# All stores of two input projections move from SyncE's queue to ScalarE's

## The chip, the cores and the metric

The kernel runs on one core of a Trainium2 chip. A core has TensorE (matrix products, into PSUM), VectorE, ScalarE and GpSimd for elementwise work, and SyncE (SP), which here only begins DMAs. ScalarE can begin DMAs too. The metric is the device time of one execution in microseconds (us). Before the change the median of 3 runs is 3293.2 us (3289.35 to 3299.78).

## The reference

A two-layer encoder over two requests of 512 and 2048 tokens, model width 1024, float32. Each layer has one input projection, two mixers, gates, one output projection and a layer norm:

```
even: qa,ka,va,qb,kb,vb,ga,gb = split(x @ w_in)
      a = windowed attention with sinks(qa,ka,va);  b = dilated attention, 3 patterns(qb,kb,vb)
      y = concat(a * silu(ga), b * silu(gb)) @ w_out
odd:  qc,kc,vc,qd,id,zf,zb,gc,gd = split(x @ w_in)
      c = 2-D neighbourhood attention(qc,kc,vc);  d = gated linear recurrence, both directions(qd,id,zf,zb)
      y = concat(c * silu(gc), norm(d) * silu(gd)) @ w_out
x <- LayerNorm(ALPHA * x + y)
```

## The kernel before

**Blocks and passes.** The 2560 tokens of both requests are five blocks of 512 (block 0 is the short request). A layer's projection handles output columns in pairs of 128-column units. `group` makes a list of work: first the pairs for blocks 0 and 1, then again for blocks 2 and 3, then for block 4 alone. Most items of the first two passes work on two blocks at once; some at the ends of a pass, and all of the last pass, on one.

**A pair.** `products` computes a pair for a block by seven products instead of eight (Strassen's scheme with shared sums). Each product takes one weight combination, split into a high part and a rest, so that three float32r matmuls stand for one float32 matmul. `next_w` keeps up to six such weight tiles (`whl`) ready. A product's PSUM accumulator is read by ScalarE (`u`, line 280, the first product) or VectorE (lines 272, 274 and those in `fin`), which frees it. There are four accumulators, two in the last pass of each layer.

**Weights.** `weights` loads a pair's weights (`wraw`, lines 178 to 181). In the first pass it builds all seven combinations: ScalarE makes the high part (line 108), GpSimd subtracts it for the rest (line 109). Four of the seven are stored to DRAM (`wk_f`, `wk_v`, line 217). In later passes these four are loaded back (line 206), and only three are built.

**Results.** `fin` ends a unit. VectorE, for gates also ScalarE's sigmoid, writes an `evo` tile; queries and keys of layer 0 are split into `evh` and the rest. Tiles go to DRAM from lines 376 and 378 (feature-major units), 393 (transposed values), 419 and 425 (values of `pair_v`; line 425 issues four stores of 80 KB for each tile). `evo` and `evh` share four buffers in layer 0, three in layer 1; a buffer is written again only when its store has landed.

**Order.** Two hand-written lists (the work list, and generators that slip loads of activations, bias tables and mixer work between products) give the order of the program. A planner then works through the program with its own estimate of durations: each engine takes the earliest instruction of the program whose inputs are ready, and the order found is fixed for each engine and queue. A DMA started by SP or ScalarE stands in that engine's order: it is issued when its inputs are ready and its completion semaphore is free. There are eight such semaphores, given out in turn over the DMAs of both queues, so that a DMA also waits for the one eight places earlier to land. The two mixers of a layer begin before the projection has ended: mixer A of layer 0 and mixer D of layer 1 run beside the last pass.

ScalarE begins only two kinds of DMA, both in the output of layer 0: the new `x` (line 998) and its transpose (line 952). All others, 2,159 of 2,199, are SP's.

Of the kernel before, what the change touches and what calls it, by code (L numbers as in the profile page):

```python
# [9 lines left out]
F32 = mybir.dt.float32  # L10
# [7 lines left out]
P = 128  # L18
# [54 lines left out]
class Trunk:  # L73
# [88 lines left out]
    def weights(self, L, pairs):  # L162


        nc = self.nc

        def load(p, first=False, kept=False):
            src = self.A[f"wv{L}"][p[1]] if p[0] == "v" else self.A[f"w{L}"][2 * p[1]:2 * p[1] + 2].unsqueeze(0)
            raws = []
            for i in range(src.shape[0]):  # L170
                raws.append(self.rp.tile([P, 2, 2, 512], F32, tag="raw", name="wraw"))
                if first:

                    part = lambda m, f, r=raws[i], i=i: nc.sync.dma_start(r[:, m, f], src[i, m, :, f * 512:f * 512 + 512])
                    part(0, 0)
                    rest.extend(lambda m=m, f=f: part(m, f) for m, f in ((0, 1), (1, 0), (1, 1)))
                elif kept:
                    nc.sync.dma_start(raws[i][:, 0].rearrange("p f c -> p (f c)"), src[i, 0])
                    nc.sync.dma_start(raws[i][:, 1, 1], src[i, 1, :, 512:])
                else:  # L180
                    nc.sync.dma_start(raws[i].rearrange("p m f c -> p m (f c)"), src[i].rearrange("m p c -> p m c"))
            return raws

        rest, kept = [], self.kept[L]
        ahead = load(pairs[0], L == 0)
        yield
        for r in rest:
            r()
        for i, p in enumerate(pairs):
            raws, ahead = ahead, None  # L190
            again = p in kept
            if not again:
                kept[p] = [[self.dram.tile([P, 2, 512], F32, name=f"wk{L}_{p[0]}{p[1]}_{j}_{n}") for n in range(4)]
                           for j in range(len(raws))]
            sums = []
            for r in raws if not again else ():
                s = self.rp.tile([P, 2, 512], F32, tag="sum", name="wsum")
                nc.vector.tensor_add(s[:, 0], r[:, 1, 0], r[:, 1, 1])
                nc.vector.tensor_sub(s[:, 1], s[:, 0], r[:, 0, 0])
                nc.vector.tensor_sub(r[:, 1, 0], r[:, 0, 0], r[:, 1, 0])  # L200
                sums.append(s)
            for n in range(7):
                for j, r in enumerate(raws):
                    w = self.wp.tile([P, 2, 512], F32R, tag="w", name="whl")
                    if again and 2 <= n < 6:
                        nc.sync.dma_start(w.bitcast(F32), kept[p][j][n - 2])
                        yield w
                        continue
                    if n == 3:
                        nc.vector.tensor_sub(r[:, 0, 1], r[:, 0, 1], sums[j][:, 1])  # L210
                    if 2 <= n < 6:
                        src = (sums[j][:, 1], r[:, 1, 0], sums[j][:, 0], r[:, 0, 1])[n - 2]
                    else:
                        src = {0: r[:, 0, 0], 1: r[:, 0, 1], 6: r[:, 1, 1]}[n]
                    self.split(w[:, 0], w[:, 1], src, nc.gpsimd)
                    if 2 <= n < 6:
                        nc.sync.dma_start(kept[p][j][n - 2], w.bitcast(F32))
                    yield w
                if n == 1 and i + 1 < len(pairs) and len(raws) == 1 and pairs[i + 1][0] == "f":
                    ahead = load(pairs[i + 1], kept=pairs[i + 1] in kept)  # L220
            if ahead is None and i + 1 < len(pairs):
                ahead = load(pairs[i + 1], kept=pairs[i + 1] in kept)
# [72 lines left out]
    def pair_fm(self, L, p, blocks, xs):  # L295
        nc, ev, nb = self.nc, self.ev, len(blocks)
# [13 lines left out]
        def fin(m, hf, accs, us):  # L310
            n, j = units[m]
# [3 lines left out]
            o = outs[m][:, :, hf]  # L315
            a = accs[0].rearrange("p (b t) -> p b t", t=256)
            u = us[0].rearrange("p (b t) -> p b t", t=256)
            if n[0] in "gz":
                c = ev.tile([P, nb, 256], F32, tag="ev", name="evc", padded_shape=[P, 2, 256])
# [40 lines left out]
            if n in ("va", "v2"):  # L360
                self.late.append(lambda o=outs[m], n=n, j=j: self.transposed(o, n, j, blocks))
            else:
                o, fm = outs[m], self.fm[L][n]
                split = n in SPLIT and not (n in ("qb", "kb") and j > 3)
                if split:
                    h = ev.tile([P, nb, 2, 256], F32, tag="eo", name="evh", bufs=4 - L, padded_shape=[P, 2, 2, 256])
                    self.split(h.bitcast(F32R), o.bitcast(F32R), o, nc.gpsimd if nb > 1 else nc.vector)
                for i, v in ((0, h), (1, o)) if split else ((0, o),):
                    dst = fm[i, j] if n in SPLIT else fm[j]
                    if n in ("qb", "kb") and j // 2 == 1:  # L370

                        for k, b in enumerate(blocks):
                            off, size = REQ[b > 0]
                            rd = dst[:, off:off + size].rearrange("p (r t) -> p r t", r=4)
                            t0 = (b * 512 - off) // 4
                            nc.sync.dma_start(rd[:, :, t0:t0 + 128], v[:, k].rearrange("p f (r t) -> p (f r) t", r=2))
                    else:
                        nc.sync.dma_start(dst[:, blocks[0] * 512:(blocks[-1] + 1) * 512], v.rearrange("p b h t -> p (b h t)"))

        self.products(1, nb * 256, scale, mul, fin)  # L380

    def transposed(self, o, n, j, blocks):

        nc = self.nc
        for i, b in enumerate(blocks):
            pt = self.acc()
            ot = o[:, i].rearrange("p h t -> p (h t)")
            for t in range(4):
                nc.tensor.transpose(pt[:, t * P:(t + 1) * P], ot[:, t * P:(t + 1) * P], self.ident)
            o2 = self.ev.tile([P, 512], F32, tag="ev", name="evt")  # L390
            nc.scalar.activation(o2, pt, AF.Copy)
            dst = self.va if n == "va" else self.vb[:, 512 + 128 * j:640 + 128 * j]
            nc.sync.dma_start(dst[b * 512:b * 512 + 512].rearrange("(j p) c -> p j c", p=P),
                              o2.rearrange("p (j c) -> p j c", c=P))

    def pair_v(self, L, g, blocks, xs):

        nc = self.nc

        def mul(accs, x):  # L400
            w = [self.next_w(), self.next_w()]
            for acc, b in zip(accs, blocks):
                xh, xl = xs[b]
                for t in range(2):
                    for k in range(4):
                        for j, (xv, wi) in enumerate(((xh, 0), (xh, 1), (xl, 0))):
                            nc.tensor.matmul(acc[:, t * 256:(t + 1) * 256], xv[:, k, x, t * P:(t + 1) * P],  # L407
                                             w[k // 2][:, wi, k % 2 * 256:(k % 2 + 1) * 256],
                                             start=(k == 0 and j == 0), stop=(k == 3 and j == 2))

        def fin(m, hf, accs, us):
            for i, b in enumerate(blocks):
                o = self.ev.tile([P, 512], F32, tag="ev", name="evv")
                nc.vector.tensor_add(o, accs[i], us[i])
                o = o.rearrange("p (t c) -> p t c", t=2)
                t0 = b * 512 + hf * 256
                if L == 0 or g:
                    dst = self.vb if L == 0 else self.vd
                    nc.sync.dma_start(dst[t0:t0 + 256, m * 256:(m + 1) * 256].rearrange("(t p) c -> p t c", p=P), o)
                    continue  # L420
                for r in range(2):
                    for h in range(2):
                        p0 = r * 64 + h * 24
                        dst = self.vc[h][t0 // 64 + r:t0 // 64 + r + 3:2, :, m * 256:(m + 1) * 256]
                        nc.sync.dma_start(dst.rearrange("t k c -> k t c"), o[p0:p0 + 40])

        self.products(len(blocks), 512, 1.0, mul, fin)

# [509 lines left out]
    def output(self, L):  # L938
# [16 lines left out]
        for t in range(NT):  # L955
# [41 lines left out]
            if L == 0:  # L997
                nc.scalar.dma_start(self.x1[t0:t0 + P, :], r)
                late.append((t, r))
                if len(late) > 1:  # L1000
                    transposed(*late.pop(0))
# [532 lines left out]
```

## Time and profile before

| | |
|---|---|
| median of 3 runs | 3293.2 us |
| the profiled execution | 3295.48 us |
| its span, first to last instruction | 3293.7 us |
| mean granted TensorE clock (1 is full speed) | 0.963 |
| busy: TensorE, VectorE, ScalarE, GpSimd | 92%, 61%, 41%, 41% |

The projection of layer 0 runs from the start to about 1010 us, beside mixer A from about 760 us. Mixer B and the output of layer 0 follow, then the projection of layer 1 from about 1580 to 2640 us, with mixer D beside it from about 2310 us, then mixers D and C and the output. An engine's idle time is put down to what ended it ("<-"). Idle time of an engine that is not the bottleneck costs nothing. In a row, a name such as `whl<-wk_f` means that `whl` is written from `wk_f`, and SPq and ACTq are the queues of SyncE and ScalarE: their DMA rows last as long as the issue does, not the transfer.

### The profile page before, as it was taken

The page shows a single profiled execution, that of the slowest core. Times are in us where ns is not written, and L with a number is a line of the kernel's source. Part 1 is how long each engine was busy: PE and PEld are TensorE (multiplying, and loading weights), DVE is VectorE, ACT ScalarE, POOL GpSimd, SP SyncE. Part 2 cuts the span into 40 slices and gives each one's busy share as a digit, 9 for nine tenths or more (in the row PEclk, how much of TensorE's full clock was granted, in tenths as well). Part 3 has the DMA queues.
Part 4 walks back from the last instruction along what each step waited for, and adds up shares of the span by engine and source line. Part 5 has one row for each costly group of instructions (what it writes and reads, how often), then busy time and mean ns, then how long its engine had stood idle before and what let it go on. Part 6 is the DMA issues. An engine that isn't in the chain of part 4 may idle for free. (4 is left out here: it accounts for less than half of the span.)

```text
span 3293.7 us, 71171 instructions
## 1 busy us (share of the span) xinstructions
PE 3037.9 (92%) x26922; PEld 2687.0 (82%) x26922; DVE 1999.2 (61%) x4484; ACT 1349.3 (41%) x3179; POOL 1349.4 (41%) x1167
## 2 busy tenths in 40 slices
PE   6999689997998998998899999999899878899998
PEld 5999689986885566677899999999889756667777
DVE  8454543255776665778654564324687988854444
ACT  4333232133555766322433332212343357775551
POOL 6446351332321110375644642113565654543224
PEclk8999899998999999999899999999999989999999
DMA  6857896699998599565855797568979784464443
GB/s 246 292 208 259 284 370 213 225 329 252 305 272 213 131 225 209 141 198 198 321 214 200 263 343 283 197 202 302 321 252 371 233 240 134 141 178 143 150 128 110
DMA packets 518043, 765.31 MB, mean 232 GB/s; under 512 B 72923, under 2 KB 331611, under 8 KB 517447
## 3 DMA queue, kind: packets, MB, share of 16 engines
q1 hardware_dynamic: 494023, 739.79, 70.6%
q10 hardware_dynamic: 23680, 20.97, 2.1%
q8 instruction: 215, 3.52, 0.4%
q14 instruction: 125, 1.02, 0.1%
HBM read 529.09 MB, written 231.54 MB: 231 GB/s over the span
## 5 line engine op out<-in xcount | busy, mean ns | idle before, releaser
L307 PE MATMUL acc<-xh,whl 128*128 128x256 f32 x7560 | 1439.8, 289 | 112.0 <-DMA whl<-wk_f 54.6
L307 PEld LDWEIGHTS acc<-xh,whl 128*128 128x128 f32 x7560 | 1220.5, 196 | 134.8 <-issue 67.6
L307 PE MATMUL acc<-xl,whl 128*128 128x256 f32 x3780 | 1086.4, 287 | 8.0 <-DVE xl L109 8.0
L109 POOL TENSOR_TENSOR whl<-wraw,whl 128x512 fp32r<-128x512 f32 x447 | 613.6, 1383 | 811.9 <-ACT whl L108 773.3
L307 PEld LDWEIGHTS acc<-xl,whl 128*128 128x128 f32 x3780 | 741.8, 196 | 9.5 <-DVE xl L109 9.5
L108 ACT ACTIVATE whl<-wraw 128x512 fp32r<-128x512 f32 x447 | 277.6, 627 | 431.1 <-PE acc L307 167.6
L978 PE MATMUL oacc<-wohl,yh 128*128 128x512 f32 x960 | 321.3, 411 | 1.5 <-ACT yh L108 1.5
L407 PE MATMUL acc<-whl,xh 128*128 128x256 f32 x1680 | 306.7, 285 | 1.4 <-POOL whl L109 1.3
L272 DVE TENSOR_TENSOR u<-acc,u 128x256 f32<-128x256 f32 (+1 forms) x279 | 146.8, 526 | 222.4 <-PE acc L307 138.4
L407 PEld LDWEIGHTS acc<-whl,xh 128*128 128x128 f32 x1680 | 262.9, 192 | 3.7 <-POOL whl L109 1.5
L407 PE MATMUL acc<-whl,xl 128*128 128x256 f32 x840 | 238.4, 284 | 0.0
L978 PEld LDWEIGHTS oacc<-wohl,yh 128*128 128x128 f32 x960 | 181.0, 191 | 46.3 <-issue 2.8
L1249 POOL TENSOR_TENSOR dK<-dK,dT 128x512 f32<-128x512 f32 x120 | 152.2, 1277 | 129.7 <-ACT dKm L1217 78.5
L978 PE MATMUL oacc<-wohl,yl 128*128 128x512 f32 x480 | 195.3, 410 | 0.0
L407 PEld LDWEIGHTS acc<-whl,xl 128*128 128x128 f32 x840 | 161.5, 192 | 0.1
L280 ACT ACTIVATE u<-acc 128x256 f32<-128x256 f32 (+1 forms) x124 | 55.8, 450 | 218.8 <-PE acc L307 189.5
L328 ACT ACTIVATE sg<-evc 128x512 f32<-128x512 f32 (+1 forms) x128 | 70.5, 551 | 181.8 <-DVE evc L320 162.0
L320 DVE TENSOR_TENSOR evc<-acc,u 128x512 f32<-128x512 f32 (+1 forms) x140 | 79.5, 570 | 90.9 <-PE acc L307 83.6
L108 ACT ACTIVATE xh<-xraw 128x768 fp32r<-128x768 f32 (+1 forms) x80 | 73.7, 945 | 143.5 <-DVE xraw L140 87.3
L1094 ACT ACTIVATE css<-css,cm 128x360 f32<-128x360 f32 (+1 forms) x160 | 92.9, 580 | 85.3 <-DVE cm L1092 84.8
L1092 DVE CUSTOM_DVE_ANT_0 css<-cs,ctab 128x360 f32<-128x360 f32 (+1 forms) x160 | 81.2, 509 | 75.0 <-PE cs L1085 72.9
L109 DVE TENSOR_TENSOR xl<-xraw,xh 128x768 fp32r<-128x768 f32 (+1 forms) x80 | 104.0, 1315 | 34.2 <-ACT xh L108 34.1
(1024 smaller groups left out, 5471.4 us busy)
## 6 DMA issues: line engine op xcount, KB each, us to landing
whl<-wk_f SPq DMA_DIRECT2D x328, 512.0 KB
wk_f<-whl SPq DMA_DIRECT2D x108, 512.0 KB
wraw<-w SPq DMA_DIRECT2D x82, 512.0 KB
wraw<-w SPq DMA_DIRECT2D x26, 1024.0 KB
whl<-wk_v SPq DMA_DIRECT2D x48, 512.0 KB
wraw<-w SPq DMA_DIRECT2D x86, 256.0 KB
vtri<-vc_d SPq DMA_DIRECT2D x60, 240.0 KB
bq<-fm_qb SPq DMA_DIRECT2D x50, 256.0 KB
```

Of the source, the lines that this page charges most:

```text
L108: nc.scalar.activation(h, src, AF.Copy)
L109: (eng_l or nc.vector).tensor_sub(l, src, h.bitcast(F32))
L272: nc.vector.tensor_add(d, a, u)
L280: nc.scalar.activation(u[i], a[i], AF.Copy, scale=scale)
L307: nc.tensor.matmul(accs[0][:, i * 256:(i + 1) * 256], w[:, wi, k * P:(k + 1) * P], xv[:, k, x], start=(k == 0 and j == 0), stop=(k == 3 an ...
L320: nc.vector.tensor_add(c, a, u)
L328: nc.scalar.activation(sg, c, AF.Sigmoid)
L407: nc.tensor.matmul(acc[:, t * 256:(t + 1) * 256], xv[:, k, x, t * P:(t + 1) * P], w[k // 2][:, wi, k % 2 * 256:(k % 2 + 1) * 256], start=( ...
L978: nc.tensor.matmul(acc, yv, wo[c][:, wi, cs], start=(c == chunks[0][0] and i == 0), stop=(c == chunks[-1][0] and i == 2))
L1092: nc.vector.tensor_tensor_reduce(ss.rearrange("p (a b) -> p a b", b=40)[:, :nr], sc[:, :nr], tb, 1.0, BIG, ALU.add, ALU.min, m[:, 0:1])
L1094: nc.scalar.activation(ss[:, :nk], ss[:, :nk], AF.Exp, scale=-1.0, bias=m[:, 0:1], accum_out=m[:, 1:2])
L1249: nc.gpsimd.tensor_mul(km, km, of(T_, nb + 1, -(nb + 1), 2, 0))
```

## The change

Six calls that store results or kept weights of the projections are made on `nc.scalar` instead of `nc.sync`. Loads stay on `nc.sync`, and so do all other stores.

```diff
@@ weights
                     if 2 <= n < 6:
-                        nc.sync.dma_start(kept[p][j][n - 2], w.bitcast(F32))
+                        nc.scalar.dma_start(kept[p][j][n - 2], w.bitcast(F32))
@@ pair_fm
-                            nc.sync.dma_start(rd[:, :, t0:t0 + 128], v[:, k].rearrange("p f (r t) -> p (f r) t", r=2))
+                            nc.scalar.dma_start(rd[:, :, t0:t0 + 128], v[:, k].rearrange("p f (r t) -> p (f r) t", r=2))
                     else:
-                        nc.sync.dma_start(dst[:, blocks[0] * 512:(blocks[-1] + 1) * 512], v.rearrange("p b h t -> p (b h t)"))
+                        nc.scalar.dma_start(dst[:, blocks[0] * 512:(blocks[-1] + 1) * 512], v.rearrange("p b h t -> p (b h t)"))
@@ transposed
-            nc.sync.dma_start(dst[b * 512:b * 512 + 512].rearrange("(j p) c -> p j c", p=P),
+            nc.scalar.dma_start(dst[b * 512:b * 512 + 512].rearrange("(j p) c -> p j c", p=P),
@@ pair_v
-                    nc.sync.dma_start(dst[t0:t0 + 256, m * 256:(m + 1) * 256].rearrange("(t p) c -> p t c", p=P), o)
+                    nc.scalar.dma_start(dst[t0:t0 + 256, m * 256:(m + 1) * 256].rearrange("(t p) c -> p t c", p=P), o)
...
-                        nc.sync.dma_start(dst.rearrange("t k c -> k t c"), o[p0:p0 + 40])
+                        nc.scalar.dma_start(dst.rearrange("t k c -> k t c"), o[p0:p0 + 40])
```

## Rows read from the trace of the kernel before

**Rows 1.** The page: busy us, share of the span and instructions of each engine.

```profile
PE 3037.9 (92%) x26922; PEld 2687.0 (82%) x26922; DVE 1999.2 (61%) x4484; ACT 1349.3 (41%) x3179; POOL 1349.4 (41%) x1167
```

**Rows 2.** Windows: stretch, its length, busy us of each engine, granted clock, DMA share, GB/s.

```profile
0.00:100.00 100.00, 66.96 (x417) 61.82 (x418) 79.72 (x93) 39.27 (x61) 60.44 (x46) 0.86 0.73 255
...
300.00:500.00 200.00, 161.03 (x1248) 156.08 (x1247) 105.84 (x170) 62.76 (x105) 93.98 (x71) 0.92 0.95 324
500.00:700.00 200.00, 199.23 (x1658) 198.71 (x1657) 68.97 (x107) 47.02 (x75) 58.68 (x41) 1.00 0.71 242
700.00:1010.00 310.00, 282.28 (x1983) 245.49 (x1982) 207.48 (x579) 148.47 (x381) 82.23 (x146) 0.94 0.96 275
...
2300.00:2640.00 340.00, 305.55 (x4133) 291.42 (x4132) 273.56 (x558) 129.76 (x277) 204.65 (x177) 0.97 0.86 296
```

**Rows 3.** Waits of TensorE, whole span: us in total, times, longest.

```profile
PE acc L307 <- DMA whl<-wk_f: 54.6, 27, 15.8
PE acc L307 <- DVE evo L343: 18.8, 7, 7.1
...
PE acc L307 <- DVE evo L345: 9.3, 5, 6.4
```

**Rows 4.** Timeline of TensorE: start us, duration; [idle before <- what ended it].

```profile
355.56 0.55 PE L307 MATMUL acc<-xh,whl 128*128 128x256 f32 x1 [15.79 <-DMA whl<-wk_f]
...
714.52 0.58 PE L307 MATMUL acc<-xh,whl 128*128 128x256 f32 x1 [6.42 <-DVE evo L345]
...
758.08 0.58 PE L307 MATMUL acc<-xh,whl 128*128 128x256 f32 x1 [7.13 <-DVE evo L343]
```

**Rows 5.** Waits of VectorE, whole span.

```profile
DVE evo L345 <- DMA fm_qb<-evh: 25.5, 7, 7.3
DVE evo L343 <- DMA fm_kb<-evh: 17.1, 3, 10.2
```

**Rows 6.** Issues of four lines: ns min/median/max, first to last start us.

```profile
L217 SPq DMA_DIRECT2D wk_f<-whl x108: 319/320/4970, 23.6 to 1902.3; - x108
...
L378 SPq DMA_DIRECT2D fm_gc<-evo x16: 319/320/2027, 1617.4 to 2639.9; - x16
...
L425 SPq DMA_DIRECT2D vc_d<-evv x80: 273/346/1524, 1796.1 to 2563.6; - x80
...
L998 ACTq DMA_DIRECT2D x_d<-res x20: 326/338/516, 1373.0 to 1577.7; - x20
```

**Rows 7.** Timeline of SP and VectorE, 704 to 758 us.

```profile
704.11 0.84 SPq L378 DMA_DIRECT2D fm_qb<-evh  x2
...
713.88 0.59 DVE L345 SCALAR_TENSOR_TENSOR evo<-acc,u 128x256 f32<-128x256 f32 x1
...
747.98 0.33 SPq L378 DMA_DIRECT2D fm_kb<-evh  x1
...
757.43 0.60 DVE L343 TENSOR_TENSOR evo<-acc,u 128x256 f32<-128x256 f32 x1 [2.93 <-DMA fm_kb<-evh]
```

**Rows 8.** Timeline of SP, 336 to 350 us.

```profile
336.16 4.97 SPq L217 DMA_DIRECT2D wk_f<-whl  x1
341.22 4.95 SPq L178 DMA_DIRECT2D wraw<-w  x1
...
348.26 1.49 SPq L206 DMA_DIRECT2D whl<-wk_f  x2
```

**Rows 9.** Timeline of ScalarE, 1434 us.

```profile
1434.60 0.34 ACTq L998 DMA_DIRECT2D x_d<-res  x1
1434.98 0.59 ACT L799 ACTIVATE cwhl<-cwt 44x512 fp32r<-44x512 f32 x1 [2.35 <-POOL res L993]
```

**Rows 10.** Waits of SP's queue, whole span.

```profile
SPq L217 <- POOL whl L109: 279.2, 102, 21.0
...
SPq L378 <- DMA whl<-wk_f: 7.0, 7, 1.5
```

**Rows 11.** Timeline of SP, 2557 us.

```profile
2557.34 6.53 SPq L425 DMA_DIRECT2D vc_d<-evv  x8
```

## The prediction

> **What bounds the kernel now.** I read the page's busy shares first: TensorE is busy 92% of the span, ScalarE and GpSimd 41% each [rows 1]. ScalarE has room on average; what matters is whether it has room where TensorE waits. The windows say where that is [rows 2]: from 500 to 700 us TensorE misses 0.8 us of 200, so there a store's queue cannot matter to it. It misses 33 us in the first 100, 39 us from 300 to 500, 28 us from 700 to 1010, and 34 us from 2300 to 2640. DMA is near its limit in the second and third of these (0.95 and 0.96).
>
> The waits of TensorE name what ends the idle time [rows 3]: the landing of a kept weight block (54.6 us in 27 waits), and VectorE's `evo` at lines 343 and 345 (18.8 and 9.3 us). Two of the latter are large, 6.42 us at 714.5 and 7.13 us at 758.1; the largest load wait is 15.79 us at 355.6 [rows 4]. Behind `evo` stand the stores: VectorE waited 25.5 and 17.1 us for the landing of `fm_qb<-evh` and `fm_kb<-evh`, whose buffers it wants back [rows 5]. So stores now cost TensorE time in two ways: they land late, and they stand in SP's queue ahead of loads.
>
> **The change part by part.** By the six lines' issue lists 527 stores leave SP (132 of line 217, 40 of 376, 220 of 378, 15 of 393, 40 of 419, 80 of 425), the first at 23.6 us, the last at 2639.9 us [rows 6]. Bytes and shapes stay; only the issuing queue changes, and with it the order that the planner writes down.
>
> *Stores that land late (gain).* The `fm_qb<-evh` pair was issued from 704.11, and `evo` could not start until 713.88; `fm_kb<-evh` was issued at 747.98, and `evo` started at 757.43, a wait that this landing ended [rows 7]. That is over 9 us from issue to reuse, with loads issued ahead of them on the same queue. On a queue that holds stores alone they can pass those loads. Bounds: 13.5 us, if both TensorE waits of rows 4 go; 0, if they land no sooner; and a loss of 5 us, if the loads that are passed land later for it (a tenth of the 54.6 us [rows 3]). Of these I take 7 us, half, because what is late next stands close by: after the wait at 758.1 TensorE needs the next kept block, and DMA is at 0.96 of its time there [rows 2].
>
> The Trainium skill, DMA: Bandwidth & Descriptors, "Issuing engines are not separate DMA queues", speaks against this gain: DMAs begun by several engines end up on the same 16 DMA engines, and beginning them elsewhere saves only the issue time. By it this term would be 0. The same page ("Queues, rings and completion order") says that each DMA engine takes turns between queue rows, which is what would let a store pass; no row of the kernel before shows the two queues side by side under a full load.
>
> *Stores ahead of loads (gain).* At 336.16 SP was held 4.97 us in issuing one `wk_f` store, right behind a store of small pieces at line 493; the weight load behind it then took 4.95 us, and the first kept load came at 348.26, too late for TensorE at 355.6 [rows 8]. With the store gone the load moves up, but it inherits the hold: the weight load that came next was held as long, and line 493 stays on SP. Bounds 0 and 5.0 us; I take 2.5.
>
> *The clock (gain).* The mean granted clock is 0.92 and 0.94 in the two stretches with these waits, 1.00 from 500 to 700 [rows 2]. Where a wait of 6 us goes, the slow restart behind it goes too. Bounds 0 and 6% of 310 us, 19 us; the two gains above are 9.5 of the 67 us idle in these stretches, a seventh, so I take 2 us.
>
> *Issue on ScalarE (loss).* One issue holds the queue 0.32 to 0.35 us at the median, and 0.34 us where ScalarE already issues stores [rows 6]: 527 x 0.34 = 179 us of ScalarE's queue. In the steady stretches TensorE hides it: ScalarE is busy 47 us of 200 from 500 to 700 [rows 2], and its work there (weight splits) is six weight buffers ahead. Cover is thin in the two stretches that work on block 4 alone, where two PSUM accumulators are left and ScalarE's copy `u` frees one of them, while a mixer wants ScalarE too: there it is busy 148 of 310 us and 130 of 340 us [rows 2]. By the code 43 and 48 stores belong to block 4. If all of their issues were on the path it would be 91 x 0.34 = 31 us, if none 0. I take 9 us, three tenths of it, since ScalarE is idle for over half of both stretches.
>
> *Waiting on ScalarE (loss).* ScalarE works in order, so a store that waits for its producer holds what is behind it. The stores at line 998 show it: at 1434.60 one waited for GpSimd, and the activation behind it, which does not need that result, stood 2.35 us [rows 9]. This is 1 of 20 stores there; at the same share 527 / 20 x 2.35 = 62 us of ScalarE, nearly all in its idle time. The stores of line 217 are the most exposed: SP waited 279.2 us for GpSimd at them, in 102 waits [rows 10]. What stands behind them on ScalarE is the split of a later weight block, for which GpSimd and then TensorE wait, five blocks later. Bounds 0 and 62; I take 3 us, most of it in the first 100 us, where TensorE has no blocks in reserve.
>
> Sum: -7 - 2.5 - 2 + 9 + 3 = +0.5 us. The profiled execution took 3295.5 us (its span is 3293.7), 2.3 us above the median of 3293.2. 3295.5 + 0.5 - 2.3 = 3293.7, about 3294: no change that could be told.
>
> **Rivals.**
> *Faster.* Stores pass the loads and SP never stands behind a producer: all `evo` waits go (18.8 + 9.3 = 28.1 us [rows 3]), and the held issue at 336 (5 us), with the clock 5 us, against 9 us of losses: -29 us, 3264. For it: SP's 279 us of waits at line 217 were time in which it could run ahead [rows 10]. Against it: its loads mostly wait for a weight buffer that TensorE still reads, and TensorE loses nothing in the steady stretches.
>
> *Slower, ScalarE held by landings.* The program gives DMAs of both queues eight completion semaphores in turn, and a DMA is issued only when the one eight places earlier has landed: SP's stores at line 378 waited 7.0 us for weight loads that have nothing to do with them [rows 10]. On ScalarE such a wait stops splits and PSUM copies until a load on the other queue has landed, and SP's next loads then wait for that store. Place: the block-4 stretches, above all the `vc_d` stores, eight of which took SP 6.53 us at 2557.34, at a time when mixer D wants ScalarE [rows 11]. Price: 91 stores in eights at 6.5 us are 74 us held; with 40% of it in TensorE's way +30 us, 3323. It decides from about 0.25 us of TensorE time per such store. For it: the last stretch is a chain of short steps over several engines. Against it: the same landings hold TensorE's own loads, so part of the wait is paid now.
>
> *No gain from the second queue.* A store lands no sooner; only the losses stay, +12 us: 3295.5 + 12 - 2.3 = 3305. For it, as a mechanism here: DMA at 0.95 and 0.96, so that what one store gains a load loses [rows 2]. The rule of the Trainium skill that is cited above comes to the same.
>
> *The change does not do what it says.* The eight semaphores tie the two queues together, so that SP runs ahead of the stores by a few DMAs at most and ScalarE's waits fall in its idle time: nothing moves, 3293.
>
> **How the numbers follow.** A measurement of this kernel tells about 0.3% from no change, 10 us, so "same" is 3283 to 3303. Chances: forecast 0.27, change without effect 0.10 (same: 0.37); faster 0.29; ScalarE held 0.24 and no gain 0.10 (slower: 0.34). The range reaches to both outer cases, 3264 and 3323, with 3 us beyond for their own spread: 3261 to 3326. The likeliest case alone spans 3276 to 3305 (its gains doubled and its losses halved, -17 us, or its gains at 0 and its losses at 12).
>
> **What would show it.** In the profile after: the 527 stores stand under ScalarE's queue with medians near 0.34 us. Gain right: VectorE's waits for `fm_qb<-evh` and `fm_kb<-evh` fall well below 42.6 us, and TensorE's for lines 343 and 345 below 28.1 us. Second gain right: the wait at about 355 us shortens by 2 to 3 us. Losses right: new waits of ScalarE behind stores in the block-4 stretches, with TensorE idle there up by some 10 us. The prediction is wrong if ScalarE's waits for unrelated landings reach TensorE, or if TensorE's idle time from 300 to 500 us falls by far more than 3 us.

## The result, and the profile after

The changed kernel takes 3317.3 us (median of 20 runs; 20 runs of the kernel before beside them: 3294.6). The ratio is 1.0064, with a 95% interval of 1.0040 to 1.0087: 21 us slower (13 to 29). That is inside the range, but on the side of the slower cases, not of the case called likeliest. The runs of most kernels here fall into two groups some 30 us apart, the longer ones at a mean granted clock about 0.01 lower (in f1 0.958 to 0.962 against 0.969 to 0.975), and their shares differ from kernel to kernel, so beside the ratio the experiments give the median of the runs within 0.6% of a kernel's fastest, the *lower group*: 3291 before (in every comparison), 3315.5 after.

The profiled execution has a span of 3319.1 us (3293.7 before). The page's busy line, which answers to [rows 1]:

```profile
PE 3043.2 (92%) x26922; PEld 2686.5 (81%) x26922; DVE 1999.1 (60%) x4499; ACT 1337.0 (40%) x3164; POOL 1352.1 (41%) x1167
```

Span less TensorE's busy time is its idle time: 255.8 us before, 275.9 after, 20.1 more. The shares of the other engines hardly move, so the loss cannot be read from them. The windows that answer to [rows 2]:

```profile
0.00:100.00 100.00, 69.30 (x428) 64.49 (x429) 77.77 (x94) 39.75 (x61) 59.68 (x46) 0.95 0.75 264
...
300.00:500.00 200.00, 151.48 (x1122) 146.94 (x1123) 99.75 (x158) 56.36 (x94) 89.05 (x67) 0.88 0.89 296
500.00:700.00 200.00, 199.18 (x1660) 198.89 (x1659) 63.01 (x99) 46.41 (x75) 55.62 (x39) 1.00 0.71 242
700.00:1010.00 310.00, 279.93 (x1956) 240.40 (x1955) 216.22 (x593) 146.13 (x372) 84.92 (x148) 0.96 0.94 276
...
2300.00:2640.00 340.00, 302.20 (x3699) 287.75 (x3699) 254.24 (x520) 123.29 (x255) 191.97 (x164) 0.96 0.87 296
```

Look at 300 to 500 us: TensorE misses 48.5 us instead of 39, and gets through 1122 matrix products instead of 1248. That is the largest single loss, and it lies outside the two block-4 stretches, whose windows lose 2 and 3 us. From 500 to 700 us, as foreseen, nothing moves. (Windows are cut by time, and late work leaves them. By the work itself: three fifths of the first projection's matrix products are done 13 us later than before, at 560.4 us instead of 547.4. The last of them ends 28 us later, at 1041.5, but mixer B, behind it, begins only 14 us later, 13 of which were lost at the three fifths already. The second projection takes 8 us more.) The waits of TensorE, for [rows 3] (total, times, longest):

```profile
PE acc L307 <- ACT u L280: 25.8, 7, 12.1
PE acc L307 <- DMA whl<-wk_f: 22.2, 17, 7.8
PE acc L307 <- DVE evo L345: 15.5, 2, 9.9
...
PE acc L307 <- DVE evo L343: 9.4, 6, 2.7
```

The load wait has fallen from 54.6 to 22.2 us, and a new first line stands above it: ScalarE's PSUM copy `u`, which does not stand among TensorE's waits in the kernel before. VectorE's waits for the two stores of [rows 5] fell from 42.6 to 14.3 us:

```profile
DVE evo L345 <- DMA fm_qb<-evh: 10.3, 3, 4.6
DVE evo L343 <- DMA fm_kb<-evh: 4.0, 1, 4.0
```

What held ScalarE? Two things. The first, in the timeline (start, duration) of SyncE, ScalarE and TensorE of the changed kernel:

```profile
322.01 0.70 SPq L493 DMA_DIRECT2D rz_d<-rp  x1
```

```profile
326.12 4.79 ACTq L376 DMA_DIRECT2D fm_qb<-evh  x1
331.02 0.63 ACT L108 ACTIVATE evh<-evo 128x512 fp32r<-128x512 f32 x1 [4.41 <-issue]
331.32 4.38 ACTq L217 DMA_DIRECT2D wk_f<-whl  x1
335.74 1.35 ACTq L376 DMA_DIRECT2D fm_qb<-evo  x1
...
340.65 0.38 ACT L280 ACTIVATE u<-acc 128x256 f32<-128x256 f32 x1 [9.01 <-issue]
```

```profile
341.09 0.58 PE L307 MATMUL acc<-xh,whl 128*128 128x256 f32 x1 [12.07 <-ACT u L280]
```

SyncE begins the store of line 493 (a bias table, written from 8 partitions). From its semaphore it lands 15.0 us later, at 337.0. Behind it two issues on *ScalarE* take 4.79 and 4.38 us instead of 0.33, and four more 0.8 to 1.4 us each; `u` stands behind all six, and TensorE stands 12.07 us. In the kernel before, the same store slowed the issue of a store and a load on SyncE [rows 8]. The second thing, 35 us later, just behind the second such store (it landed at 363.8):

```profile
374.28 0.33 ACTq L378 DMA_DIRECT2D fm_qb<-evo  x1
375.83 0.33 ACTq L378 DMA_DIRECT2D fm_qb<-evh  x1
376.20 0.84 ACT L108 ACTIVATE xh<-xraw 128x768 fp32r<-128x768 f32 x1 [12.96 <-DMA fm_qb<-evo]
```

```profile
377.08 0.96 DVE L109 TENSOR_TENSOR xl<-xraw,xh 128x768 fp32r<-128x768 f32 x1 [13.03 <-ACT xh L108]
```

```profile
389.27 0.58 PE L307 MATMUL acc<-xh,whl 128*128 128x256 f32 x1 [9.91 <-DVE evo L345]
```

The issues are short here, but each comes 0.08 us after the landing of the DMA eight places earlier, a weight load of SyncE's (by their semaphores these landed at 374.20 and 375.75). ScalarE stands for 12.96 us, VectorE behind it, and TensorE at 389. (The activations that `xh` reads were loaded by SyncE and landed at 368.5, so 7.7 of the 12.96 us at most are the stores' doing.) So a store on ScalarE waits for loads that have nothing to do with it. Going through ScalarE's timeline, I count 35 stores held until the DMA eight places earlier had landed, in three stretches, for 81 us: 25 us from 300 to 500, 35 from 700 to 1010, 22 from 2300 to 2640. All other stretches together have 4 such stores, 6 us. Nearly all of these landings are of SyncE's DMAs; in two of the 39 cases it is an earlier store of ScalarE's own, and the counts below take in both.

### The profile page after: what moved, and what is told of

Same layout as the page of the kernel before. It is cut to its first block, busy times and chain, and to the rows that moved or that the text cites. A ratio compares the mean times of both kernels' runs of the same rounds, so it can differ in the third digit from the quotient of the medians.

```text
span 3319.1 us, 70969 instructions
## 1 busy us (share of the span) xinstructions
PE 3043.2 (92%) x26922; PEld 2686.5 (81%) x26922; DVE 1999.1 (60%) x4499; ACT 1337.0 (40%) x3164; POOL 1352.1 (41%) x1167
## 5 line engine op out<-in xcount | busy, mean ns | idle before, releaser
L307 PE MATMUL acc<-xh,whl 128*128 128x256 f32 x7560 | 1446.7, 290 | 120.6 <-ACT u L280 25.8
L109 POOL TENSOR_TENSOR whl<-wsum,whl 128x512 fp32r<-128x512 f32 x66 | 92.8, 1409 | 72.2 <-ACT whl L108 38.6
```

Of the source, the lines that this page charges most:

```text
L109: (eng_l or nc.vector).tensor_sub(l, src, h.bitcast(F32))
L307: nc.tensor.matmul(accs[0][:, i * 256:(i + 1) * 256], w[:, wi, k * P:(k + 1) * P], xv[:, k, x], start=(k == 0 and j == 0), stop=(k == 3 an ...
```

## Experiments

All times in us; differences in the last column are between lower groups.

| kernel | begun by ScalarE | median (runs) | ratio to before, 95% | lower group (runs) | difference |
|---|---|---|---|---|---|
| after | all 527 | 3317.3 (20) | 1.0064 [1.0040, 1.0087] | 3315.5 (17) | +24.5 to before |
| e1_l0 | layer 0 | 3309.1 (12) | 1.0020 [0.9986, 1.0055] | 3307.6 (10) | +16.6 to before |
| e2_l1 | layer 1 | 3309.1 (12) | 1.0042 [1.0006, 1.0077] | 3307.3 (9) | +16.3 to before |
| e4_before_rz | none, bias store mended | 3277.2 (12) | 0.9936 [0.9902, 0.9971] | 3275.1 (9) | -15.9 to before |
| e3_after_rz | all, mended | 3315.0 (12) | 1.0054 [1.0010, 1.0097] | 3311.2 (8) | +36.1 to e4 |
| f1_kept | line 217 (132) | 3298.3 (12) | 0.9965 [0.9927, 1.0002] | 3272.5 (5) | -2.6 to e4 |
| f2_fm | lines 376, 378 (260) | 3296.9 (12) | 0.9999 [0.9964, 1.0033] | 3296.6 (11) | +21.5 to e4 |
| f3_val | lines 393, 419, 425 (135) | 3289.1 (12) | 0.9954 [0.9925, 0.9983] | 3287.0 (10) | +11.9 to e4 |
| f4_gps | none; all 527 by GpSimd | 3372.8 (6) | 1.0235 [1.0174, 1.0297] | 3369.7 (5) | +94.6 to e4 |
| g1_pairs | two-block items (292) | 3312.2 (12) | 1.0022 [0.9984, 1.0059] | 3283.4 (5) | +8.3 to e4 |
| g2_single | single-block items (235) | 3290.4 (12) | 0.9983 [0.9949, 1.0017] | 3289.4 (10) | +14.3 to e4 |
| g4_before_u | none, `u` on VectorE | 3275.3 (12) | 0.9923 [0.9891, 0.9954] | 3275.2 (11) | +0.1 to e4 |
| g3_after_u | all, `u` on VectorE | 3289.8 (12) | 0.9966 [0.9932, 1.0001] | 3289.8 (12) | +14.6 to g4 |

**Which layer.** The six calls take the queue by layer:

```diff
-nc.scalar.dma_start(
+(nc.scalar if L == 0 else nc.sync).dma_start(      # e1_l0; L == 1 in e2_l1
```

> Layer 0's stores on ScalarE, layer 1's back on SP. Theory A (holds at the slow rz_d stores): the loss sits between 300 and 500 us, where ScalarE is held in issuing stores behind line 493's store and then in waiting for loads' semaphores; +14 us over the kernel before (about 3309), TensorE's wait of 12 us for ScalarE's u near 341 us stays. Rival B (ScalarE's queue time, spread evenly over the 527 stores): layer 0 has 243 of them, so +10 us, with no one place. Rival C (the loss is the mixer D stretch alone): +0.

> Layer 1's stores on ScalarE, layer 0's back on SP. Theory A: +6 to +8 us (about 3302), all of it after 2440 us where vc_d stores stop ScalarE beside mixer D; 300 to 500 us as in the kernel before. Rival B: 284 of 527 stores, +12 us, spread. Rival C: +22 us.

Each layer alone costs about 16 us. That layer 1 has the whole loss is out; between the other two theories these times do not decide, though e1 keeps the wait for `u` that theory A names (11.8 us in its profile).

**Without the slow bias store.** The bias table is brought to 128 partitions (16 copies in the input) instead of 8, and each part of it is written by two stores of 128 partitions instead of one of 8, in the kernel before (e4) and after (e3):

```diff
-    rp = sb.tile(...)[:8, :80 * (r1 - r0)]
+    rp = sb.tile(...)[:, :80 * (r1 - r0)]
...
-    nc.sync.dma_start(self.rz[:, :, 80 * r0:80 * r1].rearrange("q h e -> h q e"),
-                      rp.unsqueeze(1).broadcast_to([8, 32, 80 * (r1 - r0)]))
+    for q0 in (0, 16):
+        nc.sync.dma_start(self.rz[q0:q0 + 16, :, 80 * r0:80 * r1].rearrange("q h e -> (q h) e"), rp)
...
-    a["rpb"] = f["rpb_c"][0]
+    a["rpb"] = np.concatenate([f["rpb_c"][0]] * 16, 0)
```

> The changed kernel, but each rz_d store (line 493) is made from 128 partitions in two parts instead of from 8 in one (same bytes to DRAM), so that it lands in some 4 us instead of 15. Theory A: no issue on ScalarE over 2.5 us, no 12 us wait for u; only layer 1's loss stays, so +7 us over the kernel e4 (about 3282 if e4 is 3275). Rival B: still +22 us over e4.

> The kernel before with the same rz_d stores from 128 partitions. Theory A: TensorE's load waits of 15.8 us at 355 and 7.4 us at 378 shrink to some 3 us together; -15 to -20 us, about 3275. Rival B: these waits are DMA rate, not the slow store; 3294, no change.

The stores of the table now land in 6 to 8 us instead of 14 to 16. The kernel before gains 16 us by it, as theory A had it, and is faster than either kernel of this study. But the changed kernel gains 4 us only: the cost of the move is not smaller without the slow store, it is 36 us instead of 24.5. Theory A, that this store makes the loss, falls; it is one way in which ScalarE is held, and where it is taken away the next one decides. TensorE's waits in e4 and then e3:

```profile
PE acc L307 <- DMA whl<-wk_f: 31.3, 18, 5.5
```

```profile
PE acc L307 <- DMA whl<-wk_f: 22.0, 28, 2.6
...
PE acc L307 <- ACT u L280: 15.1, 6, 8.8
```

In e4 no `u` of ScalarE stands among them. The largest one of e3, in the timelines of its SyncE, ScalarE and TensorE:

```profile
736.72 0.60 SPq L522 DMA_DIRECT2D atab<-vt_d  x1
...
745.51 0.33 ACTq L378 DMA_DIRECT2D fm_kb<-evh  x1
748.83 0.33 ACTq L378 DMA_DIRECT2D fm_kb<-evo  x1
749.33 0.63 ACT L108 ACTIVATE evh<-evo 128x512 fp32r<-128x512 f32 x1 [10.99 <-DMA atab<-vt_d]
749.87 0.37 ACT L280 ACTIVATE u<-acc 128x256 f32<-128x256 f32 x1
...
750.29 0.58 PE L307 MATMUL acc<-xh,whl 128*128 128x256 f32 x1 [8.76 <-ACT u L280]
```

The `evh` at 749.33 does not read `atab`. It stands behind a store that could go only when a piece of `atab`, begun by SyncE at 736.72, had landed (12.0 us later, at 748.75).

**Which stores, and which engine.** On the mended kernel, ScalarE (f1 to f3) or GpSimd (f4) begins only these:

```diff
-nc.sync.dma_start(kept[p][j][n - 2], ...)     # f1_kept: line 217
+nc.scalar.dma_start(kept[p][j][n - 2], ...)
...
-nc.sync.dma_start(                            # f2_fm: 376, 378; f3_val: 393, 419, 425
+nc.scalar.dma_start(
...
-nc.sync.dma_start(                            # f4_gps: all six
+nc.gpsimd.dma_start(
```

> Only the kept weights (line 217, 132 stores) are begun by ScalarE, on the kernel with the bias store from 128 partitions (3277 us with all stores on SyncE, 3315 with all on ScalarE). Theory S (ScalarE is held at a store until the DMA eight places earlier, of either queue, has landed, and TensorE waits for the PSUM copies behind it): in the trace with all stores on ScalarE such holds were 48 us at the feature-major stores (lines 376 and 378), 25 us at the values (393, 419, 425) and 0 at line 217, which waits only for GpSimd. So no loss here: 3272 to 3283. Rival O (the loss comes with the number of moved stores, by the new order and the issue time): 132 of 527, 38 x 0.25 = +10, 3287.

> Only the feature-major stores (lines 376 and 378, 260 of 527) are begun by ScalarE, on the same kernel. Theory S: two thirds of the holds, 48 of 73 us: +25, about 3302, with new TensorE waits for u at line 280 near 350 and 750 us. Rival O: 260 of 527, +19, 3296. Rival P (stores that pass loads make the loads late, whoever begins them): waits for the kept load would grow over those with all stores on SyncE (31.5 us).

> Only the values (lines 393, 419, 425; 135 of 527) are begun by ScalarE, on the same kernel. Theory S: a third of the holds, 25 of 73 us, most of it beside mixer D: +10 to +13, about 3288, and nothing changed before 2300 us. Rival O: 135 of 527, +10, 3287.

> All six stores are begun by GpSimd's queue, on the same kernel. The program gives GpSimd's DMAs eight completion semaphores of their own, so stores and loads no longer wait for each other's landings, and ScalarE begins none of them. Theory S: the loss of 38 us goes, but for what GpSimd's issues cost (not seen in any trace yet): 3262 to 3290. Rival P (stores that pass loads make the loads late): as with ScalarE, 3305 to 3320, with longer waits of TensorE for the kept load.

In the lower groups f1 to f3 came out as theory S has them: 132 stores cost nothing, 260 cost 21.5 us, 135 cost 12. For f2 and f3 rival O forecast nearly the same, so only f1 tells the two apart, and there the measure matters: by the ratios f1 lies 10 us above e4, by the medians 21. The profile of f1 (an execution of 3299 us) speaks for theory S: the first projection ends at 1000.0 us (1002.5 in e4) and the second takes 1067.9 us (1075.5), so nothing is lost where the moved stores are issued; it loses 38 us in mixer B, where none of them is (last section). Rival P is not borne out for ScalarE: TensorE's wait for kept loads is 23.7 us in f2, against 31.3 in e4. With f4 both theories miss. GpSimd is kept busy by each issue, 132 of them at line 217 at 570 ns in the median, and its own work is the rest of the weights, so TensorE waits for weights:

```profile
L217 POOL DMA_DIRECT2D wk_f<-whl x108: 531/570/747, 26.8 to 1957.3; - x108
```

```profile
PE acc L307 <- DMA whl<-wk_f: 60.5, 26, 9.1
PE acc L307 <- ACT whl L108: 27.8, 25, 6.2
```

GpSimd's busy time is 1637.5 us there, 278 more than in e4. Beside a cost of that size f4 cannot tell what separate semaphores are worth, nor whether stores pass loads: it decides nothing.

**Where they stand.** On the mended kernel, by the blocks of an item:

```diff
-nc.scalar.dma_start(                                         # lines 376, 378, 393, 419, 425 of e3
+(nc.scalar if len(blocks) == 2 else nc.sync).dma_start(      # g1_pairs (line 217 on ScalarE)
+(nc.scalar if len(blocks) == 1 else nc.sync).dma_start(      # g2_single (line 217 on SyncE)
```

> On the kernel with the bias store from 128 partitions, ScalarE begins all kept weights, and the results of items that work on two blocks; results of single-block items stay on SyncE. That is 292 of 527 stores on ScalarE. In the trace with all 527 there, 29 of the 31 holds by a foreign landing (68 of 73 us) stood at single-block items (near 355, 388, 440, 745 to 990 and 2517 to 2569 us), 2 (5 us) here. Theory S (ScalarE held by landings): next to no loss against 3277, so 3268 to 3282. Rival O (loss by number moved): 292 of 527, 38 x 0.55 = +21, 3298.

> The complement: on the same kernel ScalarE begins only the results of single-block items, 235 of 527; kept weights and all results of two blocks stay on SyncE. Theory S: nearly the whole loss of 38 us, +30 to +38, 3307 to 3315, with new TensorE waits for ScalarE's u. Rival O: 235 of 527, +17, 3294.

By the lower groups theory S is right in the order of the two and wrong in their size; by the medians the order is the other way (3312 for g1, 3290 for g2), so this rests on the lower groups. g1 has 3 us of holds and loses 8 us, not 0; g2 has 80 us of them (some 56 for landings of SyncE's DMAs, 22 for ScalarE's own earlier stores) and loses 14, not 30 to 38, less than a fifth. The two parts together make 23 of the 36 us, and f1 to f3 together 31.

**Whether it goes through the copy `u`.** Line 280 on VectorE, with all stores on ScalarE (g3) or none (g4):

```diff
-            nc.scalar.activation(u[i], a[i], AF.Copy, scale=scale)
+            nc.vector.tensor_scalar(u[i], a[i], scale, None, ALU.mult)
```

> All 527 stores on ScalarE, on the same kernel, and the PSUM copy u of line 280 is made by VectorE instead of ScalarE, so that a held ScalarE no longer keeps a PSUM accumulator from TensorE by this copy (its other work is still held). Theory S: TensorE's 15.2 us of waits for ScalarE's u go, and a part of the 7.4 us more for VectorE's u; against the kernel with the same copy on VectorE and all stores on SyncE the loss falls from 38 to 15 to 25 us. Rival (the holds of ScalarE don't reach TensorE by this copy, the loss is in loads or in the new order): it stays near 38.

> The control: all stores on SyncE, on the same kernel, with the copy u of line 280 on VectorE. TensorE waited 0 us for ScalarE's u there, so nothing is gained; VectorE gets 124 copies of about 0.5 us. All theories: 3277 to 3287.

As theory S has it, at the small end: the copy costs nothing to move where ScalarE is free (g4 stands with e4), and where ScalarE begins the stores the loss falls from 36 to 15 us. So 21 of the 36 us go when one copy of 0.4 us no longer stands behind stores. In g3 TensorE waits next to nothing for it (15.1 us in e3):

```profile
PE acc L307 <- DVE u L280: 1.4, 3, 0.7
```

The stores on ScalarE are held about as often as in e3 (30 holds in g3, 58 us; 31 in e3, 73 us); what changed by the edit is what stands behind them. (The planner's order is new in g3 too.)

## Why the prediction was right or wrong

*The forecast.* Its sum was +0.5 us, measured are +21. That lies in the range, but by a rival, not by the sum: the case called ScalarE held by landings happened (3323 was its time). Its mechanism was right; that its time comes near is in part luck, since its place and its share were not (see the last term). By the terms:

*Stores that land late, -7.* The cause was read rightly, VectorE's waits for these two stores fell by 28 us. At TensorE the two `evo` lines fell from 28.1 only to 24.9 us, since VectorE now comes late for another reason: the `evo` that TensorE waits for at 389.27 stands behind ScalarE. The store itself lands hardly sooner: over the 527 stores the median from issue to landing is 4.4 us after and 4.6 before. Whether VectorE waits less because stores are issued earlier, or because it comes later itself, was not separated. The Trainium skill, DMA: Bandwidth & Descriptors, "Issuing engines are not separate DMA queues", says that beginning DMAs on several engines saves only the time of the issue. These landings agree with it.

*Stores ahead of loads, -2.5.* This is the first step that failed: "it inherits the hold: the weight load that came next was held as long". What is held while the slow store lands is the next issue on either queue, not SyncE's alone: here it was ScalarE's, for 9 us, with TensorE's accumulator behind it. The load wait went down further than said (32 us), but part of the fall is TensorE coming later to the load, and 25.8 us of `u` stand against it.

*The clock, -2.* From 300 to 500 us it went from 0.92 to 0.88, with the idle time; over the span it is 0.967 against 0.963, but TensorE's busy time for the same work rose by 5 us. Nothing gained.

*Issue on ScalarE, +9.* At the median 0.34 us as said, and 221 us in all instead of 179, because 42 issues take over 0.6 us, two of them over 4. The 132 issues of f1 cost nothing in its lower group, so issues by themselves seem covered.

*Waiting on ScalarE, +3.* This is the term that was mis-sized. I took it from a place with one wait in 20 stores [rows 9], and said that nearly all falls into ScalarE's idle time. The row that bore on it was [rows 10], SyncE's waits for foreign landings at line 378; I put it into a rival with the right mechanism, and gave that its place in block 4. There it would have 74 us of holds and 40% of them in TensorE's way. The holds are 81 us, three tenths of them from 300 to 500 us, and g2 shows less than a fifth of such holds reaching TensorE. The 8 us of g1 come almost without such holds; ScalarE waiting for producers, or the new order, could make them, and no run separates these.

What the runs leave open: why all stores cost 14 us more than g1 and g2 added up. In the profiles, e3 loses 11 us to e4 in layer 1 between 1600 and 2050 us, which neither g1 nor g2 does, and 18 us behind the second projection's last product (674 us against 656; g2 667, g1 653), where no moved store is issued; no run takes that apart. The new order that the planner finds is a part of every variant and was not tested by itself. Also untested is a program in which SyncE's and ScalarE's queues have separate semaphores.

## What to carry to other kernels

Before a DMA moves to a computing engine's queue, look not at how busy that engine is but at what stands behind each issue in its order, and at what the issue itself can wait for: the landing of other queues' DMAs as well as its own producer. A busy share of 41% did not help where a PSUM copy of 0.4 us stood behind a store. If stores must move, move those behind which nothing is urgent (line 217, free of cost in the lower group), or take the urgent work off the engine first (line 280; even then 15 us were lost). The gain here lay in neither, but in the bias store that held the issues behind it, 16 us.

## What was not expected of the hardware

A store from 8 partitions landed after 14 to 16 us and stretched issues on the *other* queue to 4.79 and 4.38 us. What was issued behind it landed behind it, on the other queue too: the `wk_f` store that ScalarE began at 325.52 landed at 338.38 us, 12.9 us later, when the bias store had landed at 337.0. Written from 128 partitions the same table lands in 6 to 8 us (e3 and e4).

TensorE's granted clock fell to its lower level (0.50, 1.2 GHz) for 75 us at the start of mixer B in the profiled executions of f1 and e1, and not in those of the other kernels. Windows of f1 (stretch, length, busy us of each engine, clock, DMA share, GB/s):

```profile
1070.00:1090.00 20.00, 19.20 (x105) 11.42 (x103) 17.59 (x70) 14.96 (x46) 3.00 (x16) 1.00 0.48 126
1090.00:1110.00 20.00, 17.83 (x81) 9.94 (x80) 8.86 (x46) 10.17 (x43) 0.98 (x3) 0.82 0.17 53
1110.00:1130.00 20.00, 20.00 (x78) 13.14 (x79) 6.63 (x38) 9.59 (x36) 1.22 (x2) 0.50 0.27 79
```

and two of these stretches in e4, at about the same points of the work:

```profile
1070.00:1090.00 20.00, 19.16 (x103) 11.31 (x101) 17.97 (x70) 15.15 (x47) 3.02 (x16) 1.00 0.51 129
...
1110.00:1130.00 20.00, 20.00 (x156) 13.71 (x156) 12.92 (x75) 16.87 (x73) 2.45 (x4) 1.00 0.57 160
```

Before it fell TensorE was busy 19.2 of 20 us at the full clock, and e4 was no different there. At the lower level it gets through 78 products where e4 has 156, and it is busy without a break until the clock rises again. Mixer B begins at the same time in f1 and e4 and ends 38 us later in f1. Why the clock fell in these two executions, and whether moved stores make that more frequent, no run shows.
